# Feed-forward elementwise work moved from GpSimd to VectorE, and the product down in three parts instead of four

## The chip, the core and the metric

One core of a Trainium2 chip runs the whole program. The metric is device time in microseconds (us) of one execution; lower is better. The engines are named as the profile names them: PE is TensorE (matmuls), PEld its weight load, DVE is VectorE, ACT is ScalarE, POOL is GpSimd, SP is SyncE, which issues the loads.

## The reference, cut to what matters

A transformer of four layers, D = 1024 features, 512 latent and 128 context tokens (640 token columns in all, fp32). Each layer is a token mixer followed by a feed-forward part, and only the latter is touched here:

```
h  = (rms_norm(x) * g) * (1 + scale) + shift        # scale, shift differ for latent and context tokens
y  = silu(h @ w_gate) * (h @ w_up)                  # 1024 -> 2816 features, 22 tiles of 128
x += gate * (y @ w_down)                            # 2816 -> 1024
```

## The kernel before, in words

**Storage.** Activations lie feature-major: a tile has 128 features on the partitions and the 640 tokens as columns. The columns are handled as two halves of 320 (`COLS`). Every fp32 operand of a product is split into a rounded part and a rest (`hh`/`hl`, `whi`/`wlo`, `ah`/`al`), and each product is three matmuls: rounded x rounded, rounded x rest, rest x rounded. Each split costs one ACT instruction (the rounding copy) and one two-operand subtraction (the rest).

**gate and up.** The two products of one pair of feature tiles (i and i + 11) are computed by a Strassen-like scheme with seven block products instead of eight. Its operands on the activation side are made once per layer by `make_b` (L625 to L682): `scaled` (L610) writes x times its gain into `raw`, L656 multiplies by the inverse norm, L608 and L673 form differences and sums, L645/L648 (ACT) round, L649/L608 form the rests. The names T1 to T4, "11", "21" and "22" are these operands. On the weight side `make_a` (L684) loads four blocks of 128x512 and forms the sums S1 to S4 (L696). `block` (L699) splits one weight block (`two`: ACT L318, rest L319) and issues its 12 matmuls of 128x320 into a PSUM tile `big`, of which there are six. `gate_up` (L708) is one "mat": the seven blocks, in steps (`yield`), with additions of PSUM to SBUF between them (L722), silu on ACT (L730), the product gate times up (L732, L735), and the split of the result into `ah`, `al` (L760, and L608 through `sub`).

**down.** The 11 pairs are worked off in parts (`PAIRS`). Of each part first all its mats run, then the product down over this part's features for all eight output tiles d, in `feat`: 3 matmuls x 2 column halves for each of the part's feature tiles, accumulated in two PSUM tiles, after which `residual` (L603, three DVE instructions for each d) adds them to x. A part of three pairs has six feature tiles, so its weights for one d are 768 columns, read as a block of 512 and one of 256. The last part goes through `halves_first`, which also feeds the statistics of the next norm (`stat`).

**What sets the order.** In `rest` the mats overlap: while one mat runs, the first step of the next is issued early (`ahead`), but not across the end of a part:

```
for m in range(2 * i0, 2 * i1):
    ...
    if 0 < m < 2 * i1 - 1:
        ahead(m + 1)
```

The tile framework then orders the instructions of every engine by its own simulated timeline (`schedule_with_timeline_sim=True`); each engine works off its own list in that order. Buffers of one tag are a ring: a tile waits until the tile that held its buffer is done with. The ring "a" (tiles of 128x640) holds `raw`, t3 and later `ah`/`al`. There are four `raw` weight buffers (`slot`), into which SP loads.

**Which engine does the two-operand work.** DVE does most of it. POOL does, in the feed-forward part: the two differences `more`, four differences for T1 and four for T4 in `make_b`, the rests of T4 (`eng=nc.gpsimd`), the sums S3 and S4 of every mat, the rests of four weight blocks of each of the first two mats (`eng = nc.vector if i else nc.gpsimd`), three of the four products gate times up of every pair (L735), and both rests `al` of every pair. `scaled` also uses POOL (L621, one tensor operand) for six of eight tiles d, and outside the feed-forward part `weights` gives every second rest to POOL; both stay as they are.

Of the kernel before, what the change touches and what calls it, by code (L numbers as in the profile page):

```python
# [8 lines left out]
F32 = mybir.dt.float32  # L9
F32R = mybir.dt.float32r  # L10
AF = mybir.ActivationFunctionType
ALU = mybir.AluOpType
AX = mybir.AxisListType

P = 128
D = 1024
ND = 8
NL = 512
NP = 128
T = 640  # L20
# [12 lines left out]
BLK = 512  # L33
SLOTS = 4
MORE = {"whi": 5, "wlo": 5, "sum": 4}
PAIRS = ((0, 3), (3, 6), (6, 9), (9, 11))
HALF = ND // 2

LAST, EDGE = 2, 2
# [223 lines left out]
class Net:  # L263
# [51 lines left out]
    def two(self, raw, eng):  # L315

        hi, lo = (self.slot(n)[:, :raw.shape[1]] for n in ("whi", "wlo"))
        self.nc.scalar.copy(hi, raw)  # L318
        eng.tensor_tensor(lo, raw, hi.bitcast(F32), ALU.subtract)  # L319
        return hi, lo  # L320
# [289 lines left out]
    def scaled(self, pool, L, halves, d, raws):  # L610

        nc = self.nc
        if d not in raws:
            raws[d] = pool.tile([P, T], F32, tag="a", name="raw", bufs=12)
        c0, c1 = COLS[halves[0]][0], COLS[halves[-1]][1]
        for c, (s0, s1) in enumerate(((0, NL), (NL, T))):
            s0, s1 = max(s0, c0), min(s1, c1)
            if s0 < s1:
                y, x, g = raws[d][:, s0:s1], self.x[:, d, s0:s1], self.mods[L][1][:, 1, d, c:c + 1]
                if len(halves) == 2:  # L620
                    nc.gpsimd.tensor_scalar(y, x, g, None, ALU.mult)  # L621
                else:
                    nc.scalar.activation(y, x, AF.Copy, scale=g)

    def make_b(self, pool, L, B, raws):  # L625

        nc = self.nc
        lo, hi = slice(0, 320), slice(320, T)  # L630
        t3 = [pool.tile([P, 2, 320], F32, tag="a", name="raw", bufs=12) for _ in range(HALF // 2)]
        slots = [self.new_act() for _ in range(ND)]
        for tag, w in (("c", T), ("d", 320)):
            slots += [[pool.tile([P, w], F32R, tag=x + tag, name=x, bufs=HALF) for x in ("hh", "hl")] for _ in range(HALF)]
        shift = self.mods[L][0][:, 24:24 + ND]
        more = pool.tile([P, ND + HALF], F32, tag="more", name="more")
        self.sub(nc.gpsimd, more[:, :ND], shift[:, :, 1], shift[:, :, 0])
        self.sub(nc.gpsimd, more[:, ND:], shift[:, HALF:, 0], shift[:, :HALF, 0])

        done = []  # L640

        def two(name, slot, c, x, bias=None, eng=nc.vector):
            h, l = (y[:, c] for y in slots[slot])
            if bias is None:
                nc.scalar.copy(h, x)  # L645
                done.append(self.sub(eng, l, x, h.bitcast(F32)))
            else:
                nc.scalar.activation(h, x, AF.Identity, bias=bias)  # L648
                done.append(eng.scalar_tensor_tensor(l, x, bias, h.bitcast(F32), ALU.add, ALU.subtract))  # L649
            B.setdefault(name, []).append((h, l))  # L650

        def raw(d, c):
            with contextlib.ExitStack() as st:
                if len(done) >= 2:
                    st.enter_context(self.tc.issue_after(done[-2].ins))
                nc.vector.tensor_tensor(raws[d][:, c], raws[d][:, c], self.rstd[:, c], ALU.mult)  # L656

        for d in range(ND):
            raw(d, lo)
            two(("11", "21")[d // HALF], d, lo, raws[d][:, lo], shift[:, d, 0:1])  # L660
            yield
        for i in range(HALF):
            for d in (i, i + HALF):
                raw(d, hi)
                p, m = raws[d][:, NL:], more[:, d:d + 1]
                nc.scalar.activation(p, p, AF.Identity, bias=m)
            a, b, t = raws[i], raws[i + HALF], t3[i // 2][:, i % 2]
            self.sub(nc.vector, t, b[:, hi], a[:, hi])
            self.sub(nc.gpsimd, a[:, hi], a[:, hi], a[:, lo])
            two("T1", i, hi, a[:, hi])  # L670
        for i in range(HALF):
            a, b, t = raws[i], raws[i + HALF], t3[i // 2][:, i % 2]
            nc.vector.tensor_tensor(a[:, lo], t, a[:, lo], ALU.add)  # L673
            two("T2", ND + i, lo, a[:, lo], shift[:, i + HALF, 0:1])
            self.sub(nc.gpsimd, b[:, lo], b[:, lo], a[:, lo])
        for i in range(HALF):
            two("T3", ND + i, hi, t3[i // 2][:, i % 2], more[:, ND + i:ND + i + 1])
        for i in range(HALF):
            two("T4", ND + HALF + i, lo, raws[i + HALF][:, lo], eng=nc.gpsimd)
        for i in range(HALF):  # L680
            two("22", i + HALF, hi, raws[i + HALF][:, hi], shift[:, i + HALF, 0:1])
        yield  # L682

    def make_a(self, L, name, i):  # L684

        nc = self.nc
        at = [WIDX[L, name, f][0] for f in (i, i + NF // 2)]
        raw = {}
        for n in ("21", "22", "11", "12"):
            raw[n] = self.slot("raw")  # L690
            nc.sync.dma_start(raw[n], self.a["wall"][at[int(n[0]) - 1] + int(n[1]) - 1])
        for n, x, y, op in (("S1", "21", "22", ALU.add), ("S2", "S1", "11", ALU.subtract),
                            ("S3", "11", "21", ALU.subtract), ("S4", "12", "S2", ALU.subtract)):
            raw[n] = self.slot("sum")
            eng = nc.vector if n in ("S1", "S2") else nc.gpsimd
            eng.tensor_tensor(raw[n], raw[x], raw[y], op)  # L696
        return raw

    def block(self, out, A, B, start, stop, eng=None):  # L699

        h, l = self.two(A, eng or self.nc.vector)
        for k, (xh, xl) in enumerate(B):
            c = slice(k * P, (k + 1) * P)
            self.mm(out, h[:, c], xh, start and k == 0, False)
            self.mm(out, h[:, c], xl, False, False)
            self.mm(out, l[:, c], xh, False, stop and k == len(B) - 1)

    def gate_up(self, fp, L, name, i, B, pair):  # L708

        nc = self.nc  # L710
        up = name == "up"
        A = self.make_a(L, name, i)

        eng = nc.vector if i else nc.gpsimd
        a, b, d = (self.ps("big")[:, :320] for _ in range(3))
        t = fp.tile([P, 3, 320], F32, tag="sv", name="sv", bufs=2)
        s1, v1, v2 = (t[:, m] for m in range(3))
        if not up:
            pair.extend(fp.tile([P, T], F32, tag="t", name="y", bufs=4) for _ in range(2))

        def add(out, x, y):
            nc.vector.tensor_tensor(out, x, y, ALU.add)  # L722

        def result(r, c, src, v=None):

            y = pair[r][:, 320 * c:320 * c + 320]
            if not up:
                if v is not None:
                    add(y, src, v)
                self.silu = nc.scalar.activation(y, src if v is None else y, AF.Silu)  # L730
            elif v is None:
                nc.vector.tensor_tensor(y, y, src, ALU.mult)  # L732
            else:
                add(v, src, v)
                nc.gpsimd.tensor_tensor(y, y, v, ALU.mult)  # L735

        self.block(a, A["11"], B["11"], True, True, eng)
        yield
        nc.scalar.copy(s1, a)
        self.block(a, A["12"], B["21"], False, True, eng)  # L740
        result(0, 0, a)
        yield
        if i == 0:
            self.block(d, A["S1"], B["T1"], True, True, eng)
        self.block(b, A["S2"], B["T2"], True, True, eng)
        add(v1, b, s1)
        if i:
            self.block(d, A["S1"], B["T1"], True, True, eng)
        self.block(b, A["S3"], B["T3"], False, True)
        yield  # L750
        add(v2, b, s1)
        result(1, 1, d, v2)
        self.block(b, A["22"], B["T4"], False, True)
        result(1, 0, b, s1)
        self.block(d, A["S4"], B["22"], False, True)
        result(0, 1, d, v1)
        if up:
            for r in (1, 0):
                hi, lo = (fp.tile([P, T], F32R, tag="a", name=n, bufs=12) for n in ("ah", "al"))
                nc.scalar.copy(hi, pair[r])  # L760
                self.sub(nc.gpsimd, lo, pair[r], hi.bitcast(F32))
                pair[r] = (hi, lo)
        yield

# [37 lines left out]
    def rest(self, L):  # L802

        nc, tc, a = self.nc, self.tc, self.a
        with tc.tile_pool(name=f"ffn{L}", bufs=1, reuse_waits="tile") as fp:
# [32 lines left out]
            next(B_steps)  # L838
            for part, (i0, i1) in enumerate(PAIRS):
                if part:  # L840
# [917 lines left out]
```

## Time and profile before

| what | value |
|---|---|
| median of 3 runs | 3245.66 us (3241.69 to 3249.45) |
| the profiled execution: its own time | 3248.49 us |
| the profiled execution: span from first to last instruction | 3246.7 us |
| mean granted clock of TensorE | 0.975 of 2.4 GHz |
| busy time PE / DVE / ACT / POOL | 3043.1 / 2170.4 / 1527.9 / 1257.4 us |
| weight blocks loaded by SP: 512 columns, and 256 columns (down alone) | x644 of 256 KB, x96 of 128 KB |

The profile is that of one execution. Its time is made of the span and 1.8 us around it. The feed-forward part runs four times, at about 405 to 885, 1185 to 1655, 2001 to 2475 and 2774 to 3243 us from the span's start; each has a start (`make_b` and the first two mats, some 50 us), then mats and products down in turn. Busy shares are averages over stages with different limits, so the stages are read one by one.

### The profile page before, as it was taken

What the parts mean: (1) busy time and instruction counts of PE and PEld (TensorE: products, weight loads), DVE (VectorE), ACT (ScalarE), POOL (GpSimd) and SP (SyncE); (2) the same over time, 40 slices, a digit from 0 to 9 for tenths busy, and PEclk for the clock granted to TensorE, in tenths of its full rate; (3) what the DMA queues carried; (4) which work ended last, traced back from release to release, by engine and by line L of the source; (5) the groups of instructions that cost most, each with busy time, mean ns of one, the idle gap of its engine ahead of it and who ended that gap; (6) DMA issues with size and microseconds to landing.
All of it is one profiled execution on the core that took longest, in us unless ns stands there. A gap on an engine that the chain in (4) does not pass through costs nothing. (4 is left out here: it accounts for less than half of the span.)

```text
span 3246.7 us, 58033 instructions
## 1 busy us (share of the span) xinstructions
PE 3043.1 (94%) x21901; PEld 2845.8 (88%) x21901; DVE 2170.4 (67%) x4166; ACT 1527.9 (47%) x3296; POOL 1257.4 (39%) x1175
## 2 busy tenths in 40 slices
PE   8998889999989989999987898999999989799999
PEld 6997879999988779999975677899998878799999
DVE  5555486766576768667668766866765775867665
ACT  4455453433356654334346665433434575534332
POOL 2453362322244454323235445432322553633322
PEclk9998999999999999999998999999999999899999
DMA  7346552233433342222311224422433111122222
GB/s 264 94 122 206 174 196 87 80 106 104 143 104 128 110 153 74 80 82 82 88 46 39 62 74 150 145 77 82 133 106 120 43 37 43 40 85 83 77 85 78
DMA packets 163640, 331.46 MB, mean 102 GB/s; under 512 B 19104, under 2 KB 49184, under 8 KB 163360
## 3 DMA queue, kind: packets, MB, share of 16 engines
q1 hardware_dynamic: 160192, 323.47, 32.3%
q8 instruction: 173, 2.83, 0.4%
q10 hardware_dynamic: 3168, 4.28, 0.4%
q14 instruction: 107, 0.88, 0.1%
HBM read 303.86 MB, written 4.28 MB: 95 GB/s over the span
## 5 line engine op out<-in xcount | busy, mean ns | idle before, releaser
L271 PE MATMUL big<-hh,whi 128*128 128x320 f32 x2720 | 829.5, 314 | 31.3 <-ACT hh L645 12.0
L271 PE MATMUL big<-hl,whi 128*128 128x320 f32 x2720 | 832.9, 312 | 9.6 <-DVE hl L649 5.3
L271 PE MATMUL big<-hh,wlo 128*128 128x320 f32 x2720 | 823.6, 311 | 0.0
L318 ACT CAST whi<-raw 128x512 fp32r<-128x512 f32 (+3 forms) x668 | 388.5, 587 | 655.3 <-PE big L271 407.7
L319 DVE TENSOR_TENSOR wlo<-raw,whi 128x512 fp32r<-128x512 f32 (+1 forms) x504 | 439.2, 874 | 207.0 <-ACT whi L318 204.6
L271 PEld LDWEIGHTS big<-hh,whi 128*128 128x128 f32 x2720 | 509.8, 190 | 47.0 <-DVE sv L722 16.7
L271 PEld LDWEIGHTS big<-hl,whi 128*128 128x128 f32 x2720 | 511.3, 189 | 19.7 <-DVE hl L649 10.6
L271 PEld LDWEIGHTS big<-hh,wlo 128*128 128x128 f32 x2720 | 509.3, 189 | 0.4
L319 DVE TENSOR_TENSOR wlo<-sum,whi 128x512 fp32r<-128x512 f32 x336 | 304.6, 911 | 75.3 <-ACT whi L318 72.5
L319 POOL TENSOR_TENSOR wlo<-raw,whi 128x512 fp32r<-128x512 f32 (+2 forms) x164 | 225.2, 1385 | 305.4 <-ACT whi L318 274.1
L318 ACT CAST whi<-sum 128x512 fp32r<-128x512 f32 x352 | 216.0, 617 | 267.7 <-PE big L271 222.2
L271 PE MATMUL big<-al,whi 128*128 128x320 f32 x1408 | 334.0, 310 | 3.2 <-POOL al L608 3.2
L271 PE MATMUL big<-ah,whi 128*128 128x320 f32 x1408 | 332.0, 311 | 1.2 <-ACT ah L760 1.2
L271 PE MATMUL big<-ah,wlo 128*128 128x320 f32 x1408 | 333.1, 310 | 0.0
L1044 POOL TENSOR_SCALAR p<-p,st 128x640 f32<-128x640 f32 (+2 forms) x256 | 199.4, 784 | 297.0 <-DVE st L1043 188.1
L696 POOL TENSOR_TENSOR sum<-raw 128x512 f32<-128x512 f32 x88 | 124.8, 1418 | 410.3 <-DMA raw<-in_wall 242.3
L735 POOL TENSOR_TENSOR y<-y,sv 128x320 f32<-128x320 f32 x132 | 146.4, 1116 | 346.1 <-DVE sv L722 321.6
L696 POOL TENSOR_TENSOR sum<-raw,sum 128x512 f32<-128x512 f32 x88 | 121.3, 1379 | 404.2 <-ACT whi L318 161.9
L603 DVE SCALAR_TENSOR_TENSOR x<-big,mod,x 128x320 f32<-128x320 f32 (+2 forms) x480 | 182.3, 432 | 107.7 <-PE big L271 107.7
L271 PEld LDWEIGHTS big<-al,whi 128*128 128x128 f32 x1408 | 239.6, 189 | 4.1 <-POOL al L608 3.7
L271 PEld LDWEIGHTS big<-ah,whi 128*128 128x128 f32 x1408 | 238.0, 188 | 4.7 <-issue 2.5
L271 PEld LDWEIGHTS big<-ah,wlo 128*128 128x128 f32 x1408 | 239.3, 189 | 0.2
(264 smaller groups left out, 6093.7 us busy)
## 6 DMA issues: line engine op xcount, KB each, us to landing
raw<-in_wall SPq DMA_DIRECT2D x644, 256.0 KB, 2.6
rawm<-in_wmod SPq DMA_DIRECT2D x176, 512.0 KB, 5.9
k<-k SPq DMA_DIRECT2D x38, 384.0 KB, 4.5
raw<-in_wall SPq DMA_DIRECT2D x96, 128.0 KB, 2.1
bias<-in_nabias SPq DMA_DIRECT2D x16, 576.0 KB, 7.2
raw<-in_wmod SPq DMA_DIRECT2D x32, 256.0 KB, 5.8
qpe<-pes SPq DMA_DIRECT2D x56, 80.0 KB, 2.1
out_y<-x ACTq DMA_DIRECT2D x8, 320.0 KB, 2.2
```

Of the source, the lines that this page charges most:

```text
L271: return self.nc.tensor.matmul(out, lhsT=lhsT, rhs=rhs, start=start, stop=stop, skip_group_check=True)
L318: self.nc.scalar.copy(hi, raw)
L319: eng.tensor_tensor(lo, raw, hi.bitcast(F32), ALU.subtract)
L603: self.last = self.nc.vector.scalar_tensor_tensor(xs, halves[b][:, p0:p1], self.mcol(L, i, d, c), xs, ALU.mult, ALU.add)
L696: eng.tensor_tensor(raw[n], raw[x], raw[y], op)
L735: nc.gpsimd.tensor_tensor(y, y, v, ALU.mult)
L1044: nc.gpsimd.tensor_scalar(p, p, rd, 1.0, ALU.mult, ALU.mult)
```

## The change

Everything that POOL did in the feed-forward part with two tensor operands is issued on DVE: the argument `eng` goes from `two` (inside `make_b`), `block` and `gate_up`. The parts are of 4, 4 and 3 pairs instead of 3, 3, 3 and 2. The ring "a" has 16 buffers instead of 12, so that a part of four pairs (four tiles `ah`/`al` each) fits. The weights of down are laid out by the same `PAIRS`, so a part of 8 feature tiles is read as two blocks of 512 columns for each d. The diff without the repeated changes of `bufs=12` to `bufs=16` (there are four) and of the argument `eng` of `block` (there are six calls):

```diff
-PAIRS = ((0, 3), (3, 6), (6, 9), (9, 11))
+PAIRS = ((0, 4), (4, 8), (8, 11))
...
-            raws[d] = pool.tile([P, T], F32, tag="a", name="raw", bufs=12)
+            raws[d] = pool.tile([P, T], F32, tag="a", name="raw", bufs=16)
...
-        self.sub(nc.gpsimd, more[:, :ND], shift[:, :, 1], shift[:, :, 0])
-        self.sub(nc.gpsimd, more[:, ND:], shift[:, HALF:, 0], shift[:, :HALF, 0])
+        self.sub(nc.vector, more[:, :ND], shift[:, :, 1], shift[:, :, 0])
+        self.sub(nc.vector, more[:, ND:], shift[:, HALF:, 0], shift[:, :HALF, 0])
...
-        def two(name, slot, c, x, bias=None, eng=nc.vector):
+        def two(name, slot, c, x, bias=None):
...
-                done.append(self.sub(eng, l, x, h.bitcast(F32)))
+                done.append(self.sub(nc.vector, l, x, h.bitcast(F32)))
...
-            self.sub(nc.gpsimd, a[:, hi], a[:, hi], a[:, lo])
+            self.sub(nc.vector, a[:, hi], a[:, hi], a[:, lo])
             two("T1", i, hi, a[:, hi])
...
-            self.sub(nc.gpsimd, b[:, lo], b[:, lo], a[:, lo])
+            self.sub(nc.vector, b[:, lo], b[:, lo], a[:, lo])
...
-            two("T4", ND + HALF + i, lo, raws[i + HALF][:, lo], eng=nc.gpsimd)
+            two("T4", ND + HALF + i, lo, raws[i + HALF][:, lo])
...
-            eng = nc.vector if n in ("S1", "S2") else nc.gpsimd
-            eng.tensor_tensor(raw[n], raw[x], raw[y], op)
+            nc.vector.tensor_tensor(raw[n], raw[x], raw[y], op)
...
-    def block(self, out, A, B, start, stop, eng=None):
+    def block(self, out, A, B, start, stop):
-        h, l = self.two(A, eng or self.nc.vector)
+        h, l = self.two(A, self.nc.vector)
...
-        eng = nc.vector if i else nc.gpsimd
...
-                nc.gpsimd.tensor_tensor(y, y, v, ALU.mult)
+                nc.vector.tensor_tensor(y, y, v, ALU.mult)
...
-                self.sub(nc.gpsimd, lo, pair[r], hi.bitcast(F32))
+                self.sub(nc.vector, lo, pair[r], hi.bitcast(F32))
```

## Rows read from the trace of the kernel before

**Rows 1.** Page, part 1: busy time (share of the span) and instructions of each engine.

```profile
PE 3043.1 (94%) x21901; PEld 2845.8 (88%) x21901; DVE 2170.4 (67%) x4166; ACT 1527.9 (47%) x3296; POOL 1257.4 (39%) x1175
```

**Rows 2.** Table by stretch: length, then busy (count) by engine, PE clock, DMA.

```profile
core 0: us, PE busy (x) PEld busy (x) DVE busy (x) ACT busy (x) POOL busy (x), PEclk, DMA share, GB/s
2001.00:2050.00 49.00, 40.49 (x319) 31.11 (x319) 43.62 (x75) 29.98 (x66) 31.64 (x25) 0.90 0.61 213
1335.00:1407.00 72.00, 71.44 (x487) 71.18 (x487) 57.25 (x84) 32.60 (x62) 26.45 (x19) 1.00 0.29 84
1413.00:1452.00 39.00, 39.00 (x268) 39.00 (x267) 19.67 (x40) 10.02 (x17) 10.03 (x7) 1.00 0.24 75
1622.00:1648.00 26.00, 23.28 (x146) 22.67 (x145) 11.94 (x26) 7.33 (x11) 6.51 (x6) 0.93 0.09 25
3214.00:3243.00 29.00, 27.08 (x171) 26.29 (x169) 9.25 (x24) 1.45 (x2) 4.52 (x4) 0.94 0.19 74
```

**Rows 3.** Chain that ended last, 2010 to 2050 us: shares by engine and line.

```profile
by line: DVE raw L656 23.6%; DVE hl L649 23.6%; PE big L271 17.4%; DMA raw<-in_wall 6.9%; DVE hl L608 6.4%; issue 5.2%; DVE raw L673 4.9%; PE sm L271 4.7%; DVE raw L608 4.2%; DVE sum L696 3.0%; DVE wlo L319 2.2%; ACT whi L318 1.5%; DVE y L7
```

**Rows 4.** Timeline of DVE, 2036 to 2042 us: start, duration, line, operation.

```profile
2037.43 0.48 DVE L608 TENSOR_TENSOR raw<-raw 128x320 f32<-128x320 f32 x1
2037.83 1.17 DVE L649 SCALAR_TENSOR_TENSOR hl<-raw,mod,hh 128x320 fp32r<-128x320 f32 x1
2038.92 1.15 DVE L673 TENSOR_TENSOR raw<-raw 128x320 f32<-128x320 f32 x1
2039.99 0.54 DVE L649 SCALAR_TENSOR_TENSOR hl<-raw,more,hh 128x320 fp32r<-128x320 f32 x1
```

**Rows 5.** Timeline of POOL, same stretch (x2: two instructions, merged).

```profile
2037.12 2.60 POOL L608 TENSOR_TENSOR raw<-raw 128x320 f32<-128x320 f32 x2 [2.50 <-DVE raw L608]
```

**Rows 6.** Timeline of DVE, 2008 to 2013 us.

```profile
2009.48 0.69 DVE L319 TENSOR_TENSOR wlo<-sum,whi 128x512 fp32r<-128x512 f32 x1
```

**Rows 7.** Timeline of POOL, same stretch.

```profile
2007.43 4.59 POOL L621 TENSOR_SCALAR raw<-x,moda 128x128 f32<-128x128 f32 x3
```

**Rows 8.** Groups by line, DVE, 2001 to 2050 us: busy, mean ns | idle before.

```profile
L656 DVE TENSOR_TENSOR raw<-raw,rstd 128x320 f32<-128x320 f32 x16 | 12.0, 769 | 0.0
L649 DVE SCALAR_TENSOR_TENSOR hl<-raw,mod,hh 128x320 fp32r<-128x320 f32 x16 | 10.6, 660 | 0.4 <-ACT hh L648 0.4
L649 DVE SCALAR_TENSOR_TENSOR hl<-raw,more,hh 128x320 fp32r<-128x320 f32 x4 | 4.0, 999 | 0.0
L608 DVE TENSOR_TENSOR hl<-raw,hh 128x320 fp32r<-128x320 f32 x4 | 4.0, 989 | 0.0
L673 DVE TENSOR_TENSOR raw<-raw 128x320 f32<-128x320 f32 x4 | 3.2, 812 | 0.0
```

**Rows 9.** Groups by line, POOL, same stretch.

```profile
L608 POOL TENSOR_TENSOR raw<-raw 128x320 f32<-128x320 f32 x8 | 9.6, 1212 | 7.5 <-DVE raw L608 5.9 <-DVE raw L673 1.7
L608 POOL TENSOR_TENSOR hl<-raw,hh 128x320 fp32r<-128x320 f32 x4 | 4.2, 1066 | 1.2 <-ACT hh L645 1.2
L319 POOL TENSOR_TENSOR wlo<-sum,whi 128x512 fp32r<-128x512 f32 x3 | 4.0, 1336 | 2.2 <-ACT whi L318 2.2
L696 POOL TENSOR_TENSOR sum<-raw 128x512 f32<-128x512 f32 x2 | 2.7, 1366 | 0.6 <-DVE wlo L319 0.6
```

**Rows 10.** Groups by line and form, DVE, whole kernel.

```profile
L319 DVE TENSOR_TENSOR wlo<-raw,whi 128x512 fp32r<-128x512 f32 x408 | 383.8, 944 | 134.8 <-ACT whi L318 132.7
L319 DVE TENSOR_TENSOR wlo<-sum,whi 128x512 fp32r<-128x512 f32 x336 | 304.6, 911 | 75.3 <-ACT whi L318 72.5 <-PE sm L271 1.4
```

**Rows 11.** Timeline of PE, layers 1 and 3, product down of the last part.

```profile
1627.90 0.56 PE L271 MATMUL big<-al,whi 128*128 128x320 f32 x2 [2.12 <-POOL al L608]
3218.99 0.68 PE L271 MATMUL big<-al,whi 128*128 128x320 f32 x2 [1.09 <-POOL al L608]
```

**Rows 12.** Waits of PE, whole kernel: us in total, times, longest.

```profile
PE big L271 <- ACT hh L645: 12.0, 4, 4.0
PE big L271 <- DVE sv L722: 11.6, 16, 2.1
```

More of the change, by code (lines that the diff above doesn't have):

```diff
@@ L630, in make_b @@
         lo, hi = slice(0, 320), slice(320, T)
-        t3 = [pool.tile([P, 2, 320], F32, tag="a", name="raw", bufs=12) for _ in range(HALF // 2)]
+        t3 = [pool.tile([P, 2, 320], F32, tag="a", name="raw", bufs=16) for _ in range(HALF // 2)]
         slots = [self.new_act() for _ in range(ND)]
@@ L645, in two @@
                 nc.scalar.copy(h, x)
-                done.append(self.sub(eng, l, x, h.bitcast(F32)))
+                done.append(self.sub(nc.vector, l, x, h.bitcast(F32)))
             else:
                 nc.scalar.activation(h, x, AF.Identity, bias=bias)
-                done.append(eng.scalar_tensor_tensor(l, x, bias, h.bitcast(F32), ALU.add, ALU.subtract))
+                done.append(nc.vector.scalar_tensor_tensor(l, x, bias, h.bitcast(F32), ALU.add, ALU.subtract))
             B.setdefault(name, []).append((h, l))
@@ L734, in result @@
                 add(v, src, v)
-                nc.gpsimd.tensor_tensor(y, y, v, ALU.mult)
-        self.block(a, A["11"], B["11"], True, True, eng)
+                nc.vector.tensor_tensor(y, y, v, ALU.mult)
+        self.block(a, A["11"], B["11"], True, True)
         yield
         nc.scalar.copy(s1, a)
-        self.block(a, A["12"], B["21"], False, True, eng)
+        self.block(a, A["12"], B["21"], False, True)
         result(0, 0, a)
@@ L743, in gate_up @@
         if i == 0:
-            self.block(d, A["S1"], B["T1"], True, True, eng)
-        self.block(b, A["S2"], B["T2"], True, True, eng)
+            self.block(d, A["S1"], B["T1"], True, True)
+        self.block(b, A["S2"], B["T2"], True, True)
         add(v1, b, s1)
         if i:
-            self.block(d, A["S1"], B["T1"], True, True, eng)
+            self.block(d, A["S1"], B["T1"], True, True)
         self.block(b, A["S3"], B["T3"], False, True)
@@ L758, in gate_up @@
             for r in (1, 0):
-                hi, lo = (fp.tile([P, T], F32R, tag="a", name=n, bufs=12) for n in ("ah", "al"))
+                hi, lo = (fp.tile([P, T], F32R, tag="a", name=n, bufs=16) for n in ("ah", "al"))
                 nc.scalar.copy(hi, pair[r])
-                self.sub(nc.gpsimd, lo, pair[r], hi.bitcast(F32))
+                self.sub(nc.vector, lo, pair[r], hi.bitcast(F32))
                 pair[r] = (hi, lo)
```

## The prediction, made before the changed kernel ran

> **What bounds the kernel now.** I read the page first: PE is busy 94% of the span, DVE 67%, POOL 39% [rows 1]. So a faster DVE or POOL is worth only what PE waits for them, and the question is where. The table by stretch answers that [rows 2]. In the middle of a part's mats (1335 to 1407 us) PE is busy 71.4 of 72 us, in a product down of three pairs (1413 to 1452) 39.0 of 39. There nothing can be gained, whatever the other engines do. Two stretches are different. The start of a feed-forward part (2001 to 2050 us, layer 2) has PE busy 40.5 of 49 us, at a granted clock of 0.90, while DVE is busy 43.6 us. The product down of the last part, with two pairs, has 23.3 of 26 us at 0.93 in layer 1 and 27.1 of 29 at 0.94 in layer 3.
>
> Which engine holds the start? The chain that ended last answers: between 2010 and 2050 us the lines L656, L649, L608 and L673, all DVE, are about two thirds of it, PE under a quarter [rows 3]. So the start runs at DVE's pace, and the time of one DVE instruction counts there.
>
> That time is of two kinds. In the timeline the same operation (128x320, two tensors) takes 0.48 or 0.54 us, and beside a POOL subtraction 1.15 or 1.17 us [rows 4, 5]: DVE stands still for about as long as POOL's instruction still has to go. Beside POOL's `scaled` (L621, one tensor) a DVE subtraction keeps its 0.69 us [rows 6, 7]. So the instructions that leave POOL are those that hold DVE, and what stays there does not.
>
> **The change part by part.**
>
> *Start, DVE's time.* What it gets back: in layer 2, 16 x (0.769 - 0.48) + 16 x (0.660 - 0.54) + 4 x (0.999 - 0.54) + 4 x (0.989 - 0.48) + 4 x (0.812 - 0.48) = 4.6 + 1.9 + 1.8 + 2.0 + 1.3 = 11.7 us [rows 4, 8]. What it takes over: 8 + 4 instructions of 128x320 and 3 + 2 of 128x512 [rows 9], and one more of each of the latter two kinds that the rows leave out. In a row of busy DVE instructions the next starts about 0.08 us before the end of the one ahead (2037.43 + 0.48 against 2037.83 [rows 4]), so they cost 12 x 0.40 + 7 x 0.61 = 9.1 us. Net -2.6 us for each layer, -10 us for four. The ends: +36 us if nothing comes back, -47 us if all comes back and what is moved lies beside the chain; the timeline [rows 4 to 7] speaks for full return, the pace of DVE for full cost, so I take the difference.
>
> The page "VectorE: DVE Perf Modes" of the Trainium skill (The DRAIN you can't avoid) has it that a Vector instruction starts only when the pipe of the one before is empty. By that the moved ones would cost their full 12 x 0.48 + 7 x 0.69 = 10.6 us and the start would give back 4 us in all instead of 10; the rows show starts ahead of that end.
>
> *Start, the way through POOL.* PE waits 12.0 us, 3.0 in each layer, for a rounding (ACT L645) that itself follows a POOL subtraction of 1.21 us [rows 9, 12]. On DVE that is 0.48 us: -0.7 us a layer, -3 us in all (between 0, when the ACT queue is what holds it, and -12).
>
> *Mats.* For each pair DVE takes over four sums (0.69 each), three products (0.48) and two rests of 128x640 (about 0.83, an estimate by the columns of the 0.48 and 0.69): 5.9 us in the 24.8 us that PE takes for a pair's 168 matmuls (72 / 487 of a us each [rows 2]). It gets back most of 0.944 - 0.69 and 0.911 - 0.69 us on each of its rests [rows 6, 10], 14 a pair, 3.3 us. In the stretch of 72 us DVE is busy 57.3 us [rows 2], so even the net 2.6 x 3 pairs would leave it at 65 of 72. Cost on PE: 0. The cover is 7 us of idle DVE; were it gone, DVE would set the pace at one to one. Each new `al` waits on DVE for its rounding on ACT, and behind it stand rests and the additions out of PSUM (L722), for which PE already waits 11.6 us [rows 12]. Bounds for the mats: -8 (most of these waits vanish) to +26 us (0.3 us more in each of 88 mats).
>
> *Three parts.* The waits for L722 come to 16, about three a layer, where a part ends and no next mat has been begun; 0.7 us each [rows 12]. One end of a part less in each layer: -3 us (0 to -4). The matmuls stay the same in number. Eight residuals of three DVE instructions, eight weight blocks, their SP loads and ACT roundings fall away in each layer; they lie beside a PE that is busy 39.0 of 39 while DVE has 19.7 and ACT 10.0 [rows 2]: 0. SP is passed by nothing: its loads wait for `raw` buffers, which S4 now frees on DVE instead of POOL.
>
> *The last part.* With two pairs PE has 12 matmuls for each d before it needs the last pair, and stands: 2.12 us for POOL's `al` in layer 1 and 1.09 us in layer 3 [rows 11], and then runs a while at the lower of its two clock levels: (1 - 0.93) x 26 and (1 - 0.94) x 29 are 1.8 us each [rows 2]. Together 3.9 + 2.9 us. The last part now has three pairs, as the parts in the middle have, whose down shows no wait at all [rows 2], and `al` comes sooner too. I take -6 of these 6.8 us (0 to -7). Layers 0 and 2 have modulation matmuls at that place and no such wait: 0.
>
> Sum: -10 - 3 - 0 - 3 - 6 = -22 us. The profiled execution took 3248.5 us (a span of 3246.7 and 1.8 around it), so it would take 3226.5. The median of the runs, 3245.7, lies 2.8 us below it, so I predict **3223.5 us**.
>
> **The rivals.**
>
> *The start does not follow DVE.* ACT's order, the modulation loads or the new order that the planner makes take DVE's place, and only three parts and the last part remain: 3245.7 - 9 = 3237 us. For it: the longest waits of PE in the start name ACT [rows 12]. Against: the chain's two thirds [rows 3]. If the other gains get lost as well, in a new order of a PE list that was nearly full, it is no change, 3240 to 3250 us. A measurement of this kernel can tell about 0.2%, 6.5 us, from no change.
>
> *DVE becomes longer where it is the bound.* Place: the start, where DVE has no idle time ahead of its instructions [rows 8]. Price: the 9.1 us moved, less what comes back. With nothing back it is +36 - 12 = +24, 3270 us; with half back +13 - 12 = +1. So it decides once less than half of the 11.7 us returns, and it is slower than measurement tells at less than about a third, some 3255 us. For it: the sum of busy times would grow. Against: the 0.69 us beside POOL's one-tensor work [rows 6, 7], which shows that little contention can remain. The page "Perfetto Trace Analysis" of the Trainium skill (Optimizing Scalar/DVE Operations) speaks for this rival in its first half, that work may be taken off a saturated DVE to GpSimd, and against it in its second, that the two share a read port, so that this might not help; rows 4 and 5 agree with the second.
>
> *The start gains more.* The chain returns its 11.7 us and a good part of what is moved (sums, rests of T4) falls beside it: with half of the 9.1 us, 4 x 7.2 = 29 instead of 10, and half of the L722 waits goes too: 3245.7 - 48 = 3198 us.
>
> **How the numbers follow.** The forecast with its own bounds, 3208 to 3232 us: 0.50. Start not following, about 3237: 0.14, of which most is faster by over 0.2%. No change: 0.11. Slower, by the DVE rival: 0.12. More gain, under 3208: 0.13. That makes faster 0.75 (0.50 + 0.13 + 0.12), same 0.13, slower 0.12. The range leaves out the far end of the large gain and the slow rival: 3199 to 3247 us.
>
> **What would show it.** In the changed profile DVE's L656, L608 and L673 should stand near 0.48 us and both kinds of 512-column rests near 0.69 us in the mean; POOL should have no work in the feed-forward part but L621 and the next layer's first rests; DVE's busy time should be close to the same (some 300 us taken over, by these prices and the counts in the code, and a similar sum given back). The starts should be some 3 us shorter each with the chain still on DVE, the last down should show no wait for `al` in layers 1 and 3, and the mats should stay full. Wrong would be: a start of the same length with another engine in the chain; more or longer waits of PE for L722 or for `wlo` in the mats; a longer tail after the last down.

## The result, and the profile after

The changed kernel takes 3216.74 us (median of four runs, 3209.17 to 3217.62) against 3247.55 us before in the same session: a ratio of 0.990 with a 95% interval of 0.9877 to 0.9924. That is 31 us less where 22 were forecast; the profiled execution took 3216.05 us, with a span of 3214.0.

The page's first part, to be held against [rows 1]: POOL has half of its work left, DVE's sum is the same (2170 before), with 356 more instructions in it (484 moved to it, less 128 that fall away with the fourth part).

```profile
PE 3029.7 (94%) x21901; PEld 2841.6 (88%) x21901; DVE 2161.6 (67%) x4522; ACT 1528.5 (48%) x3264; POOL 607.1 (19%) x691
```

Why DVE's sum did not grow is for the most part in the durations; with the parts as before (run 1) it is 2196.3 us, 26 more than before. First the groups of DVE in the start of layer 2 (1989 to 2038 us), against [rows 8], then the row of the weight rests over the whole run (minimum, median and longest in ns), against [rows 10]:

```profile
L649 DVE SCALAR_TENSOR_TENSOR hl<-raw,mod,hh 128x320 fp32r<-128x320 f32 x16 | 8.6, 543 | 0.0
L656 DVE TENSOR_TENSOR raw<-raw,rstd 128x320 f32<-128x320 f32 x16 | 7.3, 483 | 0.0
L608 DVE TENSOR_TENSOR hl<-raw,hh 128x320 fp32r<-128x320 f32 x8 | 3.8, 480 | 0.0
L673 DVE TENSOR_TENSOR raw<-raw 128x320 f32<-128x320 f32 x4 | 1.9, 480 | 0.0
```

```profile
L319 DVE TENSOR_TENSOR wlo<-sum,whi x352: 672/683/694, 401.2 to 3152.5; 128x512 fp32r<-128x512 f32 x176
```

L656 fell from 0.769 to 0.483 us and L649 from 0.660 to 0.543; the rests of sums, which had a mean of 0.911 us, now lie between 0.672 and 0.694 in all of their 352. POOL's groups in layer 0's feed-forward part (405 to 870 us) are these two alone:

```profile
L621 POOL TENSOR_SCALAR raw<-x,moda 128x512 f32<-128x512 f32 (+1 forms) x4 | 5.7, 1440 | 0.2
L319 POOL TENSOR_TENSOR wlo<-raw,whi 128x512 fp32r<-128x512 f32 x1 | 1.3, 1298 | 446.7 <-ACT whi L318 446.7
```

The table by stretch, in the order of [rows 2] with its columns: the start of layer 2, four pairs' mats, a down of eight feature tiles, and the last downs of layers 1 and 3.

```profile
1989.00:2038.00 49.00, 38.12 (x309) 28.79 (x308) 39.02 (x91) 27.77 (x62) 0.00 (x0) 0.90 0.66 225
1361.00:1456.00 95.00, 95.00 (x650) 95.00 (x649) 75.69 (x136) 46.12 (x84) 0.00 (x0) 1.00 0.29 90
1463.00:1516.00 53.00, 53.00 (x364) 53.00 (x363) 25.33 (x50) 10.90 (x18) 0.00 (x0) 1.00 0.22 65
1593.00:1627.00 34.00, 34.00 (x233) 33.92 (x233) 18.14 (x37) 10.18 (x17) 1.08 (x1) 1.00 0.19 55
3171.00:3210.00 39.00, 38.97 (x266) 38.71 (x265) 14.54 (x33) 4.87 (x9) 0.00 (x0) 1.00 0.22 80
```

Mats and downs are full, and both last downs, which had 23.3 of 26 and 27.1 of 29 us, now are too. The start is not: PE still has 38 of 49 us there, though DVE does 91 instructions in 39.0 us where it did 75 in 43.6. What ends it is told by the chain of this stretch, against [rows 3], and by PE's waits in the whole run (total, times, longest), against [rows 12]:

```profile
by line: DMA rawm<-in_wmod 58.5%; PE sm L271 28.3%; PE big L271 9.5%; SPq L455 2.8%; issue 1.3%
```

```profile
PE sm L271 <- DMA rawm<-in_wmod: 27.4, 14, 4.3
PE big L271 <- ACT hh L645: 5.6, 2, 4.4
PE big L271 <- DVE sv L719: 2.4, 2, 1.5
```

The first of these rows was this before:

```profile
PE sm L271 <- DMA rawm<-in_wmod: 9.0, 5, 2.4
```

DVE has left the chain of the start of layer 2; the loads of the next layer's modulation weights (`rawm`) have taken its place. PE waited 9.0 us for them before and waits 27.4 now, while the waits for `hh` L645 fell from 12.0 to 5.6 and those for the addition out of PSUM (L722 before, L719 now) from 11.6 to 2.4. So the instructions became what was forecast, and the start of layer 2, which they were to shorten, has PE no fuller than before (38.1 of 49 us against 40.5).

Of the 32.7 us by which the span is shorter, 19.3 are idle time of PE. The other 13.4 are its busy time, 3043.1 before and 3029.7 now for the same 21901 matmuls. The causes of that part are not shown; one is to be seen in the rows of run 12, where the first matmul behind a wait takes 0.42 us and those after it 0.31.

### The profile page after: what moved, and what is told of

The parts are those of the page before. It is cut to its first block, busy times and chain, and to the rows that moved or that the text cites. A ratio compares the mean times of both kernels' runs of the same rounds, so it can differ in the third digit from the quotient of the medians.

```text
span 3214.0 us, 57273 instructions
## 1 busy us (share of the span) xinstructions
PE 3029.7 (94%) x21901; PEld 2841.6 (88%) x21901; DVE 2161.6 (67%) x4522; ACT 1528.5 (48%) x3264; POOL 607.1 (19%) x691
## 4 chain that ended last, share of the span: by engine, by line
PE 81%; DVE 8%; DMA 5%; ACT 3%; issue 1%; POOL 1%; SPq 0%; DVEq 0%; ACTq 0%; POOLq 0%
PE big L271 53%; PE sm L271 18%; PE S L271 6%; PE tp L1009 3%; DMA rawm<-in_wmod 3%; DMA k<-k 1%; PE tp L271 1%; DMA raw<-in_wall 1%; DVE st L1030 1%; ACT p L1031 1%; DVE x L603 1%; DVE wlo L319 1%; ACT pt L285 0%; DVE qs L958 0%; DVE hl L999 0%
## 5 line engine op out<-in xcount | busy, mean ns | idle before, releaser
L318 ACT CAST whi<-raw 128x512 fp32r<-128x512 f32 (+2 forms) x636 | 383.3, 607 | 709.2 <-PE big L271 554.0
L319 POOL TENSOR_TENSOR wlo<-raw,whi 128x512 fp32r<-128x512 f32 (+2 forms) x148 | 196.7, 1342 | 1634.0 <-ACT whi L318 1600.6
L319 DVE TENSOR_TENSOR wlo<-raw,whi 128x512 fp32r<-128x512 f32 (+1 forms) x488 | 325.1, 670 | 142.1 <-ACT whi L318 136.1
L319 DVE TENSOR_TENSOR wlo<-sum,whi 128x512 fp32r<-128x512 f32 x352 | 240.8, 684 | 54.5 <-ACT whi L318 52.9
L603 DVE SCALAR_TENSOR_TENSOR x<-big,mod,x 128x128 f32<-128x128 f32 (+2 forms) x384 | 146.2, 432 | 150.7 <-PE big L271 150.3
L271 PE MATMUL sm<-whi,hh 128*128 128x256 f32 (+1 forms) x770 | 225.1, 297 | 1.7 <-DVE qs L287 1.1
L271 PE MATMUL sm<-wlo,hh 128*128 128x256 f32 (+1 forms) x770 | 223.3, 292 | 0.2 <-POOL wlo L319 0.2
L271 PE MATMUL sm<-whi,hl 128*128 128x256 f32 (+1 forms) x770 | 223.1, 291 | 0.0
```

The costliest lines, as they stand in the source:

```text
L271: return self.nc.tensor.matmul(out, lhsT=lhsT, rhs=rhs, start=start, stop=stop, skip_group_check=True)
L603: self.last = self.nc.vector.scalar_tensor_tensor(xs, halves[b][:, p0:p1], self.mcol(L, i, d, c), xs, ALU.mult, ALU.add)
```

## The experiments

All ratios are to the kernel before on the same chip, with 95% intervals. Runs 1 to 4 split the change, 5 and 9 to 12 put kinds of work back or move more, 6 and 7 add POOL work that nothing reads, 8 tests the modulation loads.

### 1. The move without the parts

```diff
-PAIRS = ((0, 4), (4, 8), (8, 11))
+PAIRS = ((0, 3), (3, 6), (6, 9), (9, 11))
```

(against the changed kernel; the ring "a" has 12 buffers again)

> All two-operand work on DVE, but the parts stay at 3, 3, 3 and 2 pairs (ring a of 12). Theory (the starts run at DVE's pace, the last part's stop is shortened by a faster al, a third end of a part costs 0.7 us): the starts gain as in the changed kernel, the last part keeps part of its stop in layers 1 and 3, one more end of a part in each layer: 15 to 25 us under the kernel before, 6 to 12 us over the changed kernel. Rival (the three parts are what pays): within 7 us of the kernel before.

Measured: 3219.59 us, ratio 0.9925 [0.9907, 0.9943]. Most of the gain is there with four parts. Among PE's waits are:

```profile
PE big L271 <- DVE sv L719: 2.4, 2, 1.6
PE big L271 <- DVE al L608: 0.3, 1, 0.3
```

The stop of the last part, 2.12 and 1.09 us in [rows 11], goes with the move alone, although the last part still has two pairs.

### 2. The parts without the move

```diff
-PAIRS = ((0, 3), (3, 6), (6, 9), (9, 11))
+PAIRS = ((0, 4), (4, 8), (8, 11))
```

(against the kernel before, with 16 buffers in the ring "a")

> Parts of 4, 4 and 3 pairs, the two-operand work divided between DVE and POOL as before. Theory: the last part's stop in layers 1 and 3 goes (6 us) and one end of a part in each layer (3 us), the starts stay: 5 to 12 us under the kernel before, with the rests (wlo) of DVE still at 0.9 us in the mean. Rival: 20 us or more under the kernel before.

Measured: 3250.88 us, ratio 1.0013 [1.0000, 1.0026]: no gain, if anything a loss. PE's waits:

```profile
PE big L271 <- DVE sv L722: 17.0, 18, 1.5
```

One end of a part less in each layer did not lower the waits for L722; they rose from 11.6 to 17.0 us.

### 3 and 4. The start alone, the mats alone

Run 3 is the changed kernel with what POOL did in the mats put back: the sums S3 and S4, the products gate times up, and `al`. Run 4 is the reverse: these on DVE, and `make_b` and the rests of the first two mats as before.

```diff
-            nc.vector.tensor_tensor(raw[n], raw[x], raw[y], op)
+            (nc.vector if n in ("S1", "S2") else nc.gpsimd).tensor_tensor(raw[n], raw[x], raw[y], op)
...
-                nc.vector.tensor_tensor(y, y, v, ALU.mult)
+                nc.gpsimd.tensor_tensor(y, y, v, ALU.mult)
...
-                self.sub(nc.vector, lo, pair[r], hi.bitcast(F32))
+                self.sub(nc.gpsimd, lo, pair[r], hi.bitcast(F32))
```

> Three parts; on DVE what the start had on POOL (make_b and the rests of the first two mats), while in all mats the sums S3 and S4, the products gate times up and al stay on POOL. Theory (mats have a full PE and hide what DVE does): within 7 us of the changed kernel, DVE rests near 0.9 us in the mats without cost, the starts as short as in the changed kernel but for the first sums. Rival (the waits of PE for L722 in the mats fell from 11.6 to 2.4 us, and that relief is in the mats): 10 us or more over the changed kernel.

> Three parts; the mats' sums, products and al on DVE, while make_b and the rests of the first two mats stay on POOL. Theory: the starts are as long as before, but for the first sums; what remains is the last part, the ends of parts and some waits for L722: 8 to 16 us under the kernel before. Rival (relief in the mats): 20 us or more under it, near the changed kernel.

Measured: 3242.63 us, 0.9993 [0.9981, 1.0005] for the start, and 3228.06 us, 0.9944 [0.9927, 0.9962] for the mats. With run 2 this is a square, all with three parts:

| ratio to before | start on POOL | start on DVE |
|---|---|---|
| mats on POOL | 1.0013 (run 2) | 0.9993 (run 3) |
| mats on DVE | 0.9944 (run 4) | 0.9900 (the change) |

Down a column, moving the mats' work is worth 0.0069 and 0.0093 of 3246 us, 22 and 30 us. Along a row, moving the start's is worth 0.0020 and 0.0044, 6.5 and 14 us. The intervals of a column are far apart, those of the first row overlap a little and those of the second just don't. I had priced the start at -13 us and the mats at nothing. PE's waits in run 3:

```profile
PE big L271 <- DVE sv L719: 19.5, 20, 2.0
```

and the chain of the start of layer 2, first in run 3 (2007 to 2056 us), then in run 4 (1996 to 2045 us):

```profile
by line: DMA rawm<-in_wmod 40.3%; PE big L271 18.9%; PE sm L271 18.5%; DVE hl L649 5.6%; ACT whi L318 3.8%; DVE raw L656 3.7%; ACT L727 2.6%; DVE sum L695 2.5%; issue 2.3%; ACT hh L648 1.9%; DVE x L603 1.4%; DVE wlo L319 1.2%; SPq L455 1.2%
```

```profile
by line: DVE hl L649 23.2%; PE big L271 17.9%; DVE raw L656 16.4%; DVE sum L695 6.7%; issue 6.3%; DVE raw L673 5.8%; DMA raw<-in_wall 5.6%; DVE wlo L319 4.4%; DVE raw L608 3.4%; DVE hl L608 3.3%; DVE t L496 3.1%; DVE x L603 1.4%; ACT whi L3
```

Moving the start's work changes which engine ends the start of layer 2, with the mats on POOL or not. In the profiled executions the stretch from the start of the last attention projection to the first product down is 4.1, 0.7 and 3.3 us shorter in the change than in run 4 in layers 0, 1 and 3, and 1.5 us longer in layer 2: a gain, but no 3 us in each layer. The four come to 6.6 us, about half of the 12.4 us between these two executions (3226.4 and 3214.0 us of span); where the rest lies was not followed.

### 5. `al` back on POOL

```diff
-                self.sub(nc.vector, lo, pair[r], hi.bitcast(F32))
+                self.sub(nc.gpsimd, lo, pair[r], hi.bitcast(F32))
```

> The changed kernel with one kind of instruction put back: the two rests al of each pair (L608, 88 in all, 1.5 us and more on POOL) go to POOL again. Theory (formed after the first four runs: what pays is that POOL no longer holds DVE in the mats; in the trace of before, two DVE rests stretched to 2.07 us beside two al, and the addition that frees a PSUM bank came late): PE's waits for L722 come back to 7 us or more, 7 to 14 us over the changed kernel. Rival (the start's relief is what pays and the mats are covered): within 4 us of the changed kernel.

Measured: 3218.54 us, 0.9922 [0.9902, 0.9942]. PE's waits for L719 are 3.1 us instead of 2.4. By the ratio this is some 7 us over the change, within the intervals nothing. `al` beside the rests was my first suspect for the mats, and alone it brings back almost none of PE's waits.

### 6 and 7. Work on POOL that nothing reads

Both are run 1 with one more POOL instruction behind each `al`, whose output goes to a tile of its own: in run 6 the same subtraction of two tensors, in run 7 a multiplication of one.

```diff
                 self.sub(nc.vector, lo, pair[r], hi.bitcast(F32))
+                spare = fp.tile([P, T], F32, tag="spare", name="spare")
+                self.sub(nc.gpsimd, spare, pair[r], hi.bitcast(F32))
```

```diff
+                nc.gpsimd.tensor_scalar(spare, pair[r], 2.0, None, ALU.mult)
```

> The kernel of the first run (all on DVE, four parts) plus, behind each al on DVE, the same subtraction once more on POOL into a spare tile that nothing reads: work is added, nothing waits for it. Theory (contention: POOL's two-tensor instruction holds DVE's): the DVE rests beside it stretch past 1.3 us, PE's waits for L722 come back to 7 us or more, 6 to 14 us over the first run. Rival (what cost was the way of the data through the slower POOL): within 4 us of the first run.

> As the run before, but POOL's spare instruction has one tensor operand (a multiplication by a constant of the same 128x640). Theory: DVE's rests keep their 0.69 us beside it, as beside L621, and the time stays within 4 us of the first run. Rival (any POOL work beside DVE costs): as much over the first run as the run with the two-tensor spare.

Measured: 3229.27 us, 0.9950 [0.9931, 0.9970], with two tensors, and 3220.03 us, 0.9922 [0.9902, 0.9942], with one; run 1 without either has 0.9925. So 88 subtractions on POOL that are no part of the computation cost about 8 us (the intervals of runs 1, 6 and 7 overlap at their ends), and 88 multiplications nothing. Runs 6 and 7 are of one session, and five of run 6's six times lie above all six of run 7's. Here the rests and the spare instruction of run 6 (minimum, median and longest in ns):

```profile
L319 DVE TENSOR_TENSOR wlo<-sum,whi x352: 674/685/2066, 402.0 to 3176.1; 128x512 fp32r<-128x512 f32 x176
L608 POOL TENSOR_TENSOR spare<-y,ah x88: 1567/1917/7079, 471.8 to 3197.5; 128x640 f32<-128x640 f32 x88
```

and the same of run 7:

```profile
L319 DVE TENSOR_TENSOR wlo<-sum,whi x352: 673/685/1206, 404.2 to 3175.7; 128x512 fp32r<-128x512 f32 x176
L760 POOL TENSOR_SCALAR spare<-y x88: 1808/1977/2462, 473.0 to 3195.9; 128x640 f32<-128x640 f32 x88
```

Beside two tensors a rest of 0.69 us takes up to 2.07 and POOL's own instruction up to 7.08; beside one tensor 1.21 and 2.46. So POOL's two-tensor work slows DVE without any dependence between them.

The medians say nothing of the rests beside the spare instruction, since most of the 352 have no such neighbour. Of the 53 that begin while a multiplication of run 7 runs, 48 take 0.93 us or more. Two of them, on DVE and then POOL:

```profile
502.95 1.10 DVE L319 TENSOR_TENSOR wlo<-sum,whi 128x512 fp32r<-128x512 f32 x1
505.11 1.20 DVE L319 TENSOR_TENSOR wlo<-sum,whi 128x512 fp32r<-128x512 f32 x1
```

```profile
502.79 1.81 POOL L760 TENSOR_SCALAR spare<-y 128x640 f32<-128x640 f32 x1 [25.70 <-DVE y L732]
504.90 1.97 POOL L760 TENSOR_SCALAR spare<-y 128x640 f32<-128x640 f32 x1 [0.30 <-POOL spare L760]
```

So the expectation that the rests keep 0.69 us beside one tensor is wrong, though the time came out as it said. One tensor on POOL holds DVE too, a rest by up to 0.53 us; two tensors hold it by up to 1.39. DVE's busy time is 2196.3 us in run 1, 2217.3 in run 7 and 2285.6 in run 6, and only run 6 is slower. The cost to PE came at a place that I hadn't named, not at L719 (2.5 us of waits) but in the last parts of layers 1 and 3, and these waits are about half of the 8 us:

```profile
PE big L271 <- DVE al L608: 4.5, 2, 2.3
```

### 8. Are the modulation loads the new bound of the start?

The changed kernel, with the modulation matmuls issued no earlier than the mats behind which the program places them:

```diff
                     while done < todo * (m + 1) // len(mats):
-                        self.fill(1)
+                        with tc.issue_after(self.newest.ins):
+                            self.fill(1)
```

(`newest` is the last matmul issued; one filling step ahead of the mats instead of two)

> The changed kernel, with the modulation matmuls of the next layer held back behind the mats they are written after, so that none stand in the start. Theory A (in layers 0 to 2 the start's gain was taken by waits of PE for modulation weights, 27.4 us in all after, 9.0 before): these waits fall under 8 us, the starts of layers 0 to 2 become 3 us shorter each beyond the matmuls taken out of them, and the kernel 5 to 12 us faster than the changed one. Theory B (the start has holes anyway, held by DVE and ACT, and those matmuls filled them): the holes are waits for ACT or DVE instead, and the matmuls cost PE time in the full mats: 5 to 20 us slower than the changed one.

Measured: 3231.71 us, 0.9956 [0.9943, 0.9969], some 18 us slower than the change by the ratio. PE's waits:

```profile
PE big L271 <- ACT hh L646: 17.5, 4, 4.4
PE sm L271 <- DMA rawm<-in_wmod: 5.6, 3, 2.7
```

The waits for `rawm` fell from 27.4 to 5.6 us, and 17.5 us of waits for a rounding (L646 here, L645 elsewhere) came up in their place. Stretches of run 8's trace, compared with the change, show where the matmuls went. From the norm's first matmul to the first product down, layers 0 to 2 each have 96 modulation matmuls fewer (32 take 1.9 us), but are only 0, 5.6 and 4.6 us shorter. From there to the end of the feed-forward part they are 9.1, 6.5 and 9.1 us longer; layer 3, which has no such matmuls, differs by 0.1 us in both. So the loads are not a new cost that could be taken away: the modulation matmuls fill holes that the start has anyway, and held back they need PE's time later, in mats that are full.

### 9 to 11. Other kinds back on POOL, and more off it

Run 9 is the changed kernel with S3 and S4 on POOL, run 10 with the products gate times up on POOL (the first and the second edit of run 3, each alone). Run 11 goes further than the change: every second weight rest of the attention part goes to DVE too.

```diff
-            hi, lo = self.two(raw[:, :w], nc.gpsimd if self.flop >= 1 else nc.vector)
+            hi, lo = self.two(raw[:, :w], nc.vector)
```

> The changed kernel with the sums S3 and S4 of all mats on POOL again (88 + 88, 1.4 us each), products and al on DVE. Since al alone on POOL brought back no waits for L722 (3.1 us), theory: the sums are what holds DVE, since POOL works them off in the middle of a mat, ahead of the additions that free PSUM banks: waits for L722 of 8 us or more, 8 to 18 us over the changed kernel. Rival: it takes all three kinds together, and the sums alone leave the waits under 5 us and the time within 5 us.

> The changed kernel with the three products gate times up of each pair (L732, 132 in all, 1.1 us) on POOL again, sums and al on DVE. Theory (the sums): waits for L722 under 5 us, within 5 us of the changed kernel. Rival (the products, which follow the additions directly): 8 us or more of waits and 8 to 18 us over the changed kernel.

> The changed kernel, and outside the feed-forward part the weights' rests, of which every second is on POOL (148, 1.34 us), all on DVE too. Theory (POOL's two-tensor work holds DVE in the attention stages as well, but PE waits there for nothing that POOL's rests delay): DVE's stretched 1.0 us and more subtractions (L999, L535, L958) shrink, the time falls by 0 to 12 us. Rival (DVE's list gets longer in stages in which the softmax waits for it): 3 to 15 us slower than the changed kernel.

Measured: 3220.26 us, 0.9918 [0.9901, 0.9934]; 3219.00 us, 0.9919 [0.9903, 0.9936]; 3217.96 us, 0.9908 [0.9890, 0.9925]. No kind by itself costs more than some 7 us by its ratio, within the intervals nothing, while all three together (run 3) cost 30. PE's waits for L719 are 4.4, 2.3 and 1.4 us. So for run 9 the rival held, that the sums alone leave these waits under 5 us. And taking POOL's attention work away gains nothing. Run 9 has long rests all the same, without PE noticing:

```profile
L319 DVE TENSOR_TENSOR wlo<-sum,whi x352: 672/681/1829, 398.2 to 3152.8; 128x512 fp32r<-128x512 f32 x176
```

### 12. Two kinds together

The changed kernel with the sums and `al` on POOL, the products staying on DVE (the first and the third edit of run 3).

> The changed kernel with two kinds of the mats' work back on POOL, the sums S3 and S4 and both rests al of a pair (the products gate times up stay on DVE). Each of the two alone cost 2 to 4 us, all three kinds together 26 us. Theory: what POOL's two-tensor work takes from DVE in the mats comes out of DVE's idle time there (20 of 95 us), so it costs little until that is used up; two kinds are then near the edge: 3223 to 3232 us, PE's waits for L719 in all 5 to 12 us, between the 3.1 us with al alone and the 19.5 us with all three. Rival, the costs simply add: 3222 to 3224 us with waits for L719 under 5 us, and the 26 us belong to the products gate times up beside the others. Rival, it is the pair of sums with al that does all of it: over 3236 us with waits of 15 us or more.

Measured: 3250.36 us, ratio 1.0016 [1.0006, 1.0025]. The theory of a common reserve in DVE falls, and so does adding up; it is the last rival: these two kinds together cost the whole gain and a little more, though POOL has less to do (1006 us) than in run 3 (1166). PE's waits in the whole run, and the table by stretch for the second part's mats of layer 0:

```profile
PE big L271 <- DVE sv L719: 26.2, 23, 2.1
```

```profile
610.00:709.00 99.00, 95.93 (x652) 95.32 (x651) 81.80 (x119) 44.49 (x84) 27.76 (x19) 1.00 0.30 84
```

DVE has 17 us of idle time in these 99, so its reserve is not used up. What happens is local, and the timeline shows it: DVE, then POOL (the two `al` are merged), then PE.

```profile
666.69 0.68 DVE L319 TENSOR_TENSOR wlo<-sum,whi 128x512 fp32r<-128x512 f32 x1
667.29 1.58 DVE L732 TENSOR_TENSOR y<-y,sv 128x320 f32<-128x320 f32 x1
668.80 2.06 DVE L319 TENSOR_TENSOR wlo<-sum,whi 128x512 fp32r<-128x512 f32 x1
670.78 2.04 DVE L319 TENSOR_TENSOR wlo<-raw,whi 128x512 fp32r<-128x512 f32 x1
672.75 0.48 DVE L719 TENSOR_TENSOR sv<-big,sv 128x320 f32<-128x320 f32 x1
```

```profile
666.73 1.80 POOL L695 TENSOR_TENSOR sum<-raw 128x512 f32<-128x512 f32 x1 [1.31 <-DMA raw<-in_wall]
668.49 3.78 POOL L608 TENSOR_TENSOR al<-y,ah 128x640 fp32r<-128x640 f32 x2
```

```profile
673.28 0.42 PE L271 MATMUL big<-hh,whi 128*128 128x320 f32 x1 [1.68 <-DVE sv L719]
```

A sum and two `al` stand in a row on POOL, 5.5 us without a gap. Three DVE instructions are held in that time, by (1.58 - 0.48) + (2.06 - 0.69) + (2.04 - 0.69) = 3.8 us; the addition behind them comes late by that, its PSUM tile comes free late, and PE stands for 1.68 us. Two us or so of lateness are absorbed there (3.8 - 1.68). The same place in run 5, with `al` alone on POOL:

```profile
678.54 0.49 DVE L732 TENSOR_TENSOR y<-y,sv 128x320 f32<-128x320 f32 x1
678.94 2.07 DVE L319 TENSOR_TENSOR wlo<-sum,whi 128x512 fp32r<-128x512 f32 x1
680.94 2.06 DVE L319 TENSOR_TENSOR wlo<-raw,whi 128x512 fp32r<-128x512 f32 x1
682.92 0.48 DVE L719 TENSOR_TENSOR sv<-big,sv 128x320 f32<-128x320 f32 x1
```

```profile
678.52 3.94 POOL L608 TENSOR_TENSOR al<-y,ah 128x640 fp32r<-128x640 f32 x2 [19.49 <-PE big L271]
```

Two held instead of three, 2.75 us, and the trace has no wait of PE behind them. (PE has 32 modulation matmuls at that place, 1.94 us from 682.78 us on, which would cover a short one.) But it is not a gapless row on POOL that decides. At another place of run 12 the same three kinds of instruction stand on POOL with gaps of 1.8 and 1.2 us, and PE waits 1.54 us behind them:

```profile
532.61 1.30 POOL L695 TENSOR_TENSOR sum<-raw,sum 128x512 f32<-128x512 f32 x1 [7.28 <-DVE sum L695]
535.70 1.59 POOL L608 TENSOR_TENSOR al<-y,ah 128x640 fp32r<-128x640 f32 x1 [1.79 <-ACT ah L757]
538.48 1.56 POOL L608 TENSOR_TENSOR al<-y,ah 128x640 fp32r<-128x640 f32 x1 [1.19 <-ACT ah L757]
```

```profile
541.05 0.41 PE L271 MATMUL big<-hh,whi 128*128 128x320 f32 x1 [1.54 <-DVE sv L719]
```

What the waits have in common can be counted over the 308 additions out of PSUM into `sv` (L722 or L719) of each trace. For each, take the DVE instructions that ended in the 8 us ahead of it, and sum what each took beyond the shortest of its kind in the same trace; that is the time for which DVE was held.

| trace | held under 3 us: additions, of them with a wait of PE (us) | held 3 us or more: additions, of them with a wait of PE (us) |
|---|---|---|
| before | 252, 0 | 56, 16 (11.6) |
| run 2 | 245, 1 (0.5) | 63, 17 (16.5) |
| run 3 | 254, 6 (5.3) | 54, 14 (14.2) |
| run 12, sums and `al` | 274, 4 (4.5) | 34, 19 (21.6) |
| run 5, `al` alone | 308, 3 (3.1) | 0 |
| run 9, sums alone | 308, 6 (4.4) | 0 |
| run 10, products alone | 308, 2 (2.3) | 0 |
| the change | 308, 2 (2.4) | 0 |

PE's waits stand where DVE was held for 3 us or more within a few us, though not behind every such addition, and no kind alone ever holds it that long. Four of the other waits in run 3 and in run 12, 4.5 us, stand in the first mats of the four layers. The two bounds, 8 and 3 us, were chosen on these traces and are shown for no other kernel. In the profiled executions run 12 is 34.6 us longer than the change: 23.8 of these are the waits for L719, and 9.1 are busy time of PE (3038.8 us against 3029.7). The framework plans each kernel anew, so part of the difference between runs 5, 9 and 12 may be order; and why run 12 is slower than run 3, with less work on POOL, stays open.

## Why the prediction was right, and where its steps were wrong

The sign and the size held: 3216.7 us lies in the range and 6.8 us under the forecast, and the durations by which it was argued came out as written (0.48, 0.54, 0.69 us; 0.82 us for the 640-column rests on DVE by their own row, where the estimate was 0.83). The sum came out near for a partly wrong reason, and so in part by luck: the mats gave 22 to 30 us that were not in it, and the three parts by themselves gave nothing of the 9 that were.

**Mats, priced at 0: wrong, and the largest term.** The step said that POOL's hold on DVE is worth nothing in the mats because the stretch of 72 us showed PE busy for 71.4 of it and DVE idle for 15. It is worth 22 to 30 us (the square of runs 2 to 4), outside its lower bound of -8. The stretch that I read was a full one; the waits for L722 in [rows 12], 16 of them, were the trace of the mechanism of run 12, and I put them down to the ends of parts. Ahead of all 16 DVE was held for 3 us or more (the table of run 12). One of them follows a sum, two products and these two `al`, 7.4 us on POOL without a gap:

```profile
1276.32 3.56 POOL L608 TENSOR_TENSOR al<-y,ah 128x640 fp32r<-128x640 f32 x2
```

```profile
1280.89 0.41 PE L271 MATMUL big<-hh,whi 128*128 128x320 f32 x1 [1.02 <-DVE sv L722]
```

They fell to two by the move alone (run 1), and did not fall by the parts (run 2). PE's waits for that line explain 17 of the mats' 22 to 30 us (19.5 in run 3, 2.4 after); PE's busy time, 3043.8 us in run 3, is 14 us shorter in the change as well. In the profiled executions run 3's feed-forward parts, taken from the start of the last attention projection, are 26 us longer than the change's, 15 of them ahead of the first product down; how much of that is the sums of the first two mats, which stand in the start, and how much the plan, I did not separate. The other end of the bound, +26 us for `al` waiting on DVE, did not show: no wait for `al` is left.

**Start, priced at -13 with the way through POOL: size about right, course wrong.** By whole runs it is -6.5 with the mats on POOL and -14 with them on DVE, of which the starts show 6.6 (run 4 against the change). But "the chain still on DVE" and "3 us shorter each" are wrong: in layer 2 the chain went over to the modulation loads, as in the rival by which the start does not follow DVE, and as one of the prediction's own signs of being wrong has it (another engine in the chain of a start that is no shorter). That rival's price, nothing at all, is wrong too. Run 8 shows what the loads are: fillers of holes, behind which the roundings wait as before. Layer 3 has no modulation matmuls, and there the start and the first mats are 3.3 us shorter by the move of the start (run 4 against the change).

The page "VectorE: DVE Perf Modes" of the Trainium skill (The DRAIN you can't avoid) would have made the moved instructions cost their full time, though the same section says that a next one that is not held starts earlier. The runs show starts ahead of the end as before (in run 5's timeline 678.54 + 0.49 against the next at 678.94), but the start's end, no longer set by DVE, does not tell the two prices apart.

**Three parts -3 and the last part -6: given to the wrong edit.** Three parts alone are worth nothing (run 2); the stop for `al` does go, but by the move alone as well (run 1), and run 6 brings it back by holding DVE. Together with the move the parts may be worth 0.0025, 8 us (0.9925 without them, 0.9900 with), where the intervals overlap; that stays open.

**The rival that DVE becomes the bound** needed less than half of the held time to come back. Nearly all came back: with the parts as before (run 1) 484 more instructions, some 300 us by the prediction's prices, add 26 us to DVE's 2170. The change has 2162 because its parts also take 128 instructions off DVE.

**One tensor on POOL, priced at nothing for DVE: not wholly right.** That "what stays there does not" hold DVE was read from one instruction [rows 6, 7]. In the changed kernel none of the 27 weight rests of 512 columns that begin beside L621 is stretched, but three sums beside it are, from 0.68 to 1.10 us; and run 7 shows the hold on rests. It is too small here to reach the time.

The page "SBUF — State Buffer" of the Trainium skill (Who interferes with whom) says that a DVE instruction with two SBUF inputs contends with a GpSimd instruction that reads SBUF, and that the order of issue decides who is blocked. Runs 6 and 12 agree, and that POOL's spare subtraction took up to 7.08 us in run 6 agrees with the second half: POOL is held as well. Run 7 agrees with the first half: its multiplication reads one tensor from SBUF, and 48 of the 53 rests that begin beside it take 0.93 to 1.21 us instead of 0.69. It holds DVE for less than two tensors do (up to 0.53 us against 1.39), and the time didn't change.

## What to carry to other kernels

A profile with PE full in the middle of a stage and another engine half idle does not price contention at nothing: list all of PE's short waits by the line they wait for, and look in the timeline at what ran on POOL ahead of each. Two-tensor work on POOL beside two-tensor work on DVE hurt here where it held DVE for long within a few us ahead of an instruction that PE waits for, so add up the held time there, and test such kinds in combination and not one at a time; here any one was harmless and two of them cost the whole gain. And when the engine that holds a stage is relieved, look for work that already fills its holes before counting on the stage to shrink.

## What the runs showed of the hardware that I had not expected

- Costs of work on POOL did not add: S3 and S4 alone 0.0018 of the time over the change, `al` alone 0.0022, both 0.0116 (by the ratios 0.9918, 0.9922, 1.0016 against 0.9900).
- DVE and POOL hold each other: in run 6 a POOL subtraction with a minimum of 1.57 us took up to 7.08, and DVE's rests up to 2.07.
- A POOL instruction with one tensor, of 1.8 to 2.5 us, held DVE as well: 48 of the 53 rests of 0.69 us that began beside it took 0.93 to 1.21. It cost no time (run 7).
- Of the additions out of PSUM with DVE held for under 3 us in the 8 us ahead, none of 252 made PE wait in the kernel before; of the other 56, 16 did.
